# A [128, 128] bfloat16 identity and four columns of ones moved from the first SBUF pool to the third, in a one-core two-block transformer kernel

## The chip, the cores and the metric

The kernel runs on one core of a Trainium2 chip. The metric is the device time of one execution in microseconds. Before the change it is 2216.32 us, the median of three executions (2214.37 to 2220.98 us). Executions of one kernel lie close together, so a change of about 0.3%, some 7 us, is what a measurement of this kernel can tell from none.

TensorE multiplies a moving operand, streamed from SBUF, by a stationary operand (the weights) that was loaded into the array from SBUF before. The profile calls the two halves PE (the MATMUL) and PEld (the LDWEIGHTS), and they overlap. The notation `pm<-r,hi` names the PSUM tile that is written, then the moving operand, then the stationary one.

## The reference

Two blocks of a residual network act on 256 tokens of width 1024, in float32. Cut to what matters:

```python
def first_block(x, mem, ...):                     # depth 1
    h = x + 0.5 * rms_norm(swiglu(rms_norm(x)))                   # width 2816
    h = h + rms_norm(hybrid_mixer(rms_norm(h), w_in, ...) @ w_out)  # attention + delta rule
    h = h + rms_norm(memory_cross_attention(rms_norm(h), rms_norm(mem), ...))
    return h + 0.5 * rms_norm(swiglu(rms_norm(h)))

def second_block(x, p, ...):                      # depth 2
    for i in range(2):
        h = h + 0.5 * swiglu_2(rmsnorm(h), ...)
        h = h + hybrid_mixer_2(rmsnorm(h), w_in[i], ...)          # conv + state space
        h = h + 0.5 * swiglu_2(rmsnorm(h), ...)
        h = h + sigmoid(rmsnorm(h) @ ple_w_gate[i]) * (p[i] @ ple_w_proj[i])
    return rmsnorm(h, final_norm)
```

Nearly all the work is the products of a [256, K] activation with float32 weight matrices, 375 MB of them, each read once.

## The kernel before

**Split products.** Each float32 operand is kept as a pair of float32r tiles, a high part and the rest. `mm3` makes one 128 by 128 by 256 product from three matmuls: weights `wh` against `xh`, `wh` against `xl`, `wl` against `xh`. Each loads its own weights, `wh` twice.

**Weights.** `wunit` reads up to four [128, 256] blocks by one DMA of 512 KB into a tile `raw`, ScalarE writes the high part `hi` (L298), VectorE the rest `lo` (L299). There are four buffers of `raw`, three of `hi`, three of `lo`, of 4096 bytes a partition each, all in the pool `wp`. Block by block, `block` runs through two column halves and up to four K steps; the two halves lie 512 bytes apart, the steps 1024.

**Activations.** The tiles `s` ([128, 256] float32, 1024 bytes), `r` ([128, 2, 256] float32r, 2048 bytes: high part and rest) and `d` ([128, 2, 256] float32) are handed out by the arenas. `x[k]` in `mm3` is an `r` tile.

**Two places where the roles differ.** `preload` puts the first weights of the next projection into free `r` tiles instead of `hi` and `lo`; those matmuls read `pm<-r,r`. `proj_tok` takes the activations as the stationary operand and the weights as the moving one: `pm<-hi,r` and `pm<-lo,r`. `small_cols` multiplies by a narrow weight of 32 or 64 columns in a tile `smw`: `px<-r,smw`.

**What sets the order.** The Tile framework schedules the instructions by priorities; `AHEAD`, `PRELOAD` and `LATE` shift them. The five engines then run their queues in order.

**Where tiles lie.** The pools are laid out one behind the other in each partition of SBUF, in the order in which they are opened: `cst` (constants), `wp` (weights), `sc` (scratch), `arena` (activations), then the pools of a scope. The tiles of a pool are laid out in the order in which they are asked for, each rounded up to 32 bytes. In the built program before, by bytes in a partition: `cst` from 16512, the first `raw` at 25728, the first `hi` at 42112, the first `lo` at 54400, `sc` from 66688, the first `s` at 82240, the first `r` at 119104. All sizes in `wp` and in the arenas are multiples of 512, or pairs of 1024, so modulo 512 every weight tile lies at 128 and every arena tile at 320. This document calls the moving operand's address less the stationary one's, modulo 512, the **distance**: 192 for `pm<-r,hi` and `pm<-r,lo`, 320 for `pm<-hi,r`, 0 for `pm<-r,r`, and 0 or 256 for `px<-r,smw`, whose tile lies at 320 too.

The names that the change touches: `self.ones` (L161, four [128, 1] tiles, the moving operand of the sums of squares) and `self.identb` (L188, a [128, 128] bfloat16 identity, 256 bytes, the stationary operand in `fox` and `ssd` and for the masks of the delta rule).

Of the kernel before, what the change touches and what calls it, by code (L numbers as in the profile page):

```python
# [8 lines left out]
F32 = mybir.dt.float32  # L9
F32R = mybir.dt.float32r  # L10
BF16 = mybir.dt.bfloat16
# [4 lines left out]
P = 128  # L16
# [80 lines left out]
class Arena:  # L97


    def __init__(self, name, shape, dtype):  # L100
        self.name, self.shape, self.dtype = name, shape, dtype
        self.free, self.used, self.parts = [], {}, []
        self.n = self.peak = 0
# [33 lines left out]
class Net:  # L137
    def __init__(self, ctx, tc, a):
        self.tc, self.nc, self.a = tc, tc.nc, a
        nc = self.nc  # L140

        def pool(name, bufs, **kw):
            return ctx.enter_context(tc.tile_pool(name=name, bufs=bufs, **kw))

        self.cst = pool("cst", 1)
        self.wp = pool("wp", 3)
        self.scr, self.parts, self.pp = {}, [], []
        self.sc = pool("sc", 2)
        ap = pool("arena", 1)
        self.S = Arena("s", [P, S], F32)  # L150
        self.S.add(ap, 36)
        self.R = Arena("r", [P, 2, S], F32R)
        self.R.add(ap, 20)
        self.D = Arena("d", [P, 2, S], F32)
        self.D.add(ap, 0)
        self.pm = pool("pm", 4, space=bass.MemoryType.PSUM)
        self.px = pool("px", 4, space=bass.MemoryType.PSUM)

        self.con = self.cst.tile([P, NCON], F32, name="con")
        self.vec = self.cst.tile([P, NPACK], F32, name="vec")  # L160
        self.ones = {n: self.cst.tile([P, 1], F32, name=f"ones{n}") for n in (1, 128, 512, 1024)}  # L161
        nc.gpsimd.memset(self.ones[1], 1.0)
        for n in (128, 512, 1024):
            self.act(self.ones[n], self.ones[1], AF.Copy, scale=1.0 / n)
        self.h = self.start()
        self.ident = self.c("ident")
        nc.sync.dma_start(self.ident, a["con"][:, :P])
        self.ones_sq = self.cst.tile([P, P], F32, name="ones_sq")
        nc.gpsimd.memset(self.ones_sq, 1.0)
        self.mhalf = self.cst.tile([P, 16], F32, name="mhalf")  # L170
        self.cst.tile([P, 8], F32, name="pad")
        nc.gpsimd.memset(self.mhalf, -0.5)

    def constants(self):
        nc, a = self.nc, self.a
        nc.sync.dma_start(self.vec[:, 8:], a["pack"][:, 8:])
        nc.sync.dma_start(self.con[:, P:], a["con"][:, P:])
        tmps = [self.S.get() for _ in range(-(-NCONB // S))]
        for i, t in enumerate(tmps):
            n = min(S, NCONB - i * S)  # L180
            nc.sync.dma_start(t[:, :n], a["conb"][:, i * S:i * S + n])

        self.cb = self.cst.tile([P, NCONB], BF16, name="cb")
        for i, t in enumerate(tmps):
            n = min(S, NCONB - i * S)
            nc.gpsimd.tensor_copy(self.cb[:, i * S:i * S + n], t[:, :n])
        self.S.put(*tmps)
        self.identb = self.cst.tile([P, P], BF16, name="identb")  # L188
        nc.gpsimd.tensor_copy(self.identb, self.ident)
        self.maskT2 = self.cst.tile([P, 2, P], BF16, name="maskT2")  # L190
        nc.gpsimd.tensor_copy(self.maskT2, self.b("maskT")[:, None, :].to_broadcast([P, 2, P]))
        self.ident3 = self.b("ident3")[:96]
# [1283 lines left out]
```

## Time and profile before

| | |
|---|---|
| median of three executions | 2216.32 us |
| the profiled execution, its own time | 2218.59 us |
| its span, first instruction to last | 2216.8 us |
| PE busy | 2195.6 us (99%), 18672 matmuls |
| PEld busy | 2153.5 us (97%) |
| VectorE, ScalarE busy | 1558.2 us (70%), 1185.7 us (53%) |
| DMA | 379.44 MB, mean 171 GB/s |
| chain of work that ended last | PE 96%, VectorE 2%, ScalarE 1%, DMA 1% |

Around the span lie 1.8 us. A busy share says little for TensorE, since the matmuls overlap: one of 280 ns can follow the last after 113 ns. What tells its speed is how many start in a stretch of time: the windows view gives in brackets the instructions of each engine in each stretch, and its length by that count is the time from start to start, called the **pace** below. The timeline gives the start of each run of like instructions, and from one start to the next it gives the same.

### The profile page before, as it was taken

How to read it: one execution, taken by the hardware profiler on the slowest of the kernel's cores; microseconds unless marked ns; L12 is line 12 of the kernel's file. 1: busy time of each engine (PE TensorE's matmuls, PEld its weight loads, DVE VectorE, ACT ScalarE, POOL GpSimd, SP SyncE). 2: the span in 40 equal slices, each digit the busy share in tenths (PEclk: the TensorE clock that was granted, in tenths of full speed). 3: DMA queues.
4: the chain of work that ended last, by engine and by line, in shares of the span. 5: the costliest groups of instructions: out<-in, count | busy, mean ns of one | idle time of the engine just before them, and what ended most of it. 6: DMA issues, size and time to landing. Idle time of an engine off the chain costs nothing.

```text
span 2216.8 us, 45480 instructions
## 1 busy us (share of the span) xinstructions
PE 2195.6 (99%) x18672; PEld 2153.5 (97%) x18672; DVE 1558.2 (70%) x2608; ACT 1185.7 (53%) x2033; POOL 43.7 (2%) x54
## 2 busy tenths in 40 slices
PE   8999999999999999999999999999999999999998
PEld 8999997999999999998999999999999999999998
DVE  7756873667665766798766766676669876767666
ACT  6545633555444544567555555454457755645444
POOL 1000000000000000000000000000000000000000
PEclk9999997999999999999999999999999999999999
DMA  7565520535566556553455656656665436566563
GB/s 256 177 188 166 166 77 1 172 124 162 189 184 192 173 185 184 188 179 105 157 189 184 193 191 193 189 186 193 191 199 184 135 126 194 178 195 192 193 189 126
DMA packets 110369, 379.44 MB, mean 171 GB/s; under 512 B 12368, under 2 KB 17104, under 8 KB 110160
## 3 DMA queue, kind: packets, MB, share of 16 engines
q1 hardware_dynamic: 110160, 376.53, 53.6%
q8 instruction: 146, 2.39, 0.5%
q14 instruction: 63, 0.52, 0.1%
HBM read 375.43 MB, written 1.05 MB: 170 GB/s over the span
## 4 chain that ended last, share of the span: by engine, by line
PE 96%; DVE 2%; ACT 1%; DMA 1%; issue 0%; POOL 0%; SPq 0%; DVEq 0%; ACTq 0%; POOLq 0%
PE pm L266 84%; PE px L266 11%; PE px L269 1%; DVE lo L299 0%; DVE s L260 0%; DMA raw<-in_ffn_w_gate_dram 0%; DMA raw<-in_ple_w_gate_dram 0%; ACT hi L298 0%; DMA raw<-in_ffn_wu_dram 0%; ACT d L263 0%; PE pm L269 0%; ACT L263 0%; DVE r L260 0%; DVE w L254 0%; DVE w L260 0%
## 5 line engine op out<-in xcount | busy, mean ns | idle before, releaser
L266 PE MATMUL pm<-r,hi 128*128 128x256 f32 x10640 | 1864.0, 280 | 7.5 <-ACT hi L298 5.7
L266 PEld LDWEIGHTS pm<-r,hi 128*128 128x128 f32 x10640 | 1625.1, 189 | 9.8 <-ACT hi L298 5.7
L266 PE MATMUL pm<-r,lo 128*128 128x256 f32 x5320 | 1485.3, 279 | 0.0
L299 DVE TENSOR_TENSOR lo<-raw,hi 128x1024 fp32r<-128x1024 f32 (+1 forms) x718 | 860.9, 1199 | 488.9 <-ACT hi L298 485.6
L298 ACT CAST hi<-raw 128x1024 fp32r<-128x1024 f32 (+1 forms) x718 | 739.3, 1030 | 732.7 <-PE pm L266 576.7
L266 PEld LDWEIGHTS pm<-r,lo 128*128 128x128 f32 x5320 | 1002.1, 188 | 1.2 <-issue 0.7
L277 ACT CAST r<-w 128x256 fp32r<-128x256 f32 x136 | 54.5, 403 | 60.4 <-DVE w L254 60.3
L254 DVE TENSOR_TENSOR t<-pm,rb 128x512 f32<-128x512 f32 (+1 forms) x132 | 80.4, 635 | 0.2
L263 ACT ACTIVATE r<-s,vec 128x256 fp32r<-128x256 f32 x136 | 66.0, 504 | 21.4 <-DVE s L260 17.9
L263 ACT ACTIVATE sq<-s 128x256 f32<-128x256 f32 x152 | 60.4, 411 | 28.1 <-DVE s L254 19.8
L260 DVE SCALAR_TENSOR_TENSOR s<-pm,vec,s 128x255 f32<-128x255 f32 x144 | 68.9, 479 | 2.8
L260 DVE SCALAR_TENSOR_TENSOR r<-s,vec,r 128x256 fp32r<-128x256 f32 x136 | 65.3, 498 | 4.9 <-ACT r L263 4.4
L266 PE MATMUL px<-r,hi 128*128 128x256 f32 x384 | 66.9, 279 | 0.0
L278 DVE TENSOR_TENSOR r<-w,r 128x256 fp32r<-128x256 f32 x136 | 57.0, 421 | 8.1
L266 PEld LDWEIGHTS px<-r,hi 128*128 128x128 f32 x384 | 58.6, 189 | 0.0
L266 PE MATMUL px<-r,lo 128*128 128x256 f32 x192 | 53.5, 278 | 0.0
L414 POOL TENSOR_TENSOR rs<-rv,mhalf 128x2 f32<-128x2 f32 x26 | 23.4, 900 | 1505.0 <-DVE rv L412 1505.0
L263 ACT ACTIVATE w<-t 128x256 f32<-128x256 f32 x132 | 48.1, 409 | 7.2 <-DVE t L254 7.2
L254 DVE TENSOR_TENSOR w<-w,t 128x256 f32<-128x256 f32 x132 | 50.1, 418 | 0.3 <-ACT w L263 0.2
L266 PE MATMUL px<-d,d 128*64 128x128 f32 (+2 forms) x384 | 42.7, 291 | 0.3 <-DVE d L254 0.2
L257 DVE TENSOR_TENSOR acc<-acc,sq 128x256 f32<-128x256 f32 x94 | 39.4, 419 | 4.6 <-ACT sq L263 1.9
L263 ACT ACTIVATE d<-px,nac 128x128 f32<-128x128 f32 x128 | 36.5, 376 | 3.1 <-PE px L266 2.8
(231 smaller groups left out, 1369.2 us busy)
## 6 DMA issues: line engine op xcount, KB each, us to landing
raw<-in_w_in_dram SPq DMA_DIRECT2D x188, 512.0 KB, 3.7
raw<-in_ffn_wg_dram SPq DMA_DIRECT2D x88, 512.0 KB, 4.4
raw<-in_ffn_wu_dram SPq DMA_DIRECT2D x88, 512.0 KB, 4.3
raw<-in_ffn_wd_dram SPq DMA_DIRECT2D x80, 512.0 KB, 4.0
raw<-in_ffn_w_up_dram SPq DMA_DIRECT2D x44, 512.0 KB, 4.5
raw<-in_ffn_w_gate_dram SPq DMA_DIRECT2D x43, 512.0 KB, 4.5
raw<-in_ffn_w_down_dram SPq DMA_DIRECT2D x40, 512.0 KB, 3.8
raw<-in_m_w_out_dram SPq DMA_DIRECT2D x32, 512.0 KB, 4.3
```

Of the source, the lines that this page charges most:

```text
L254: self.nc.vector.tensor_tensor(out=out, in0=a, in1=b, op=ALU.mult)
L257: self.nc.vector.tensor_tensor(out=out, in0=a, in1=b, op=ALU.add)
L260: self.nc.vector.scalar_tensor_tensor(out=out, in0=a, scalar=s, in1=b, op0=op0, op1=op1)
L263: self.nc.scalar.activation(out, a, f, **kw)
L266: self.nc.tensor.matmul(out, lhsT=lhsT, rhs=rhs, start=start, stop=stop)
L269: self.nc.tensor.transpose(out, a, self.ident[:k, :k])
L277: nc.scalar.copy(hi, src)
L278: nc.vector.tensor_tensor(out=lo, in0=src, in1=hi, op=ALU.subtract)
L298: nc.scalar.copy(o, r)
L299: nc.vector.tensor_tensor(out=d, in0=r, in1=o, op=ALU.subtract)
L414: self.nc.gpsimd.tensor_tensor(out=r, in0=v, in1=self.mhalf[:, :2], op=ALU.pow)
```

## The change

`self.ones` and `self.identb` are asked for from `sc` instead of `cst`.

```diff
@@ -158,7 +158,7 @@
-        self.ones = {n: self.cst.tile([P, 1], F32, name=f"ones{n}") for n in (1, 128, 512, 1024)}
+        self.ones = {n: self.sc.tile([P, 1], F32, tag=f"ones{n}", name=f"ones{n}", bufs=1) for n in (1, 128, 512, 1024)}
@@ -185,7 +185,7 @@
-        self.identb = self.cst.tile([P, P], BF16, name="identb")
+        self.identb = self.sc.tile([P, P], BF16, name="identb", bufs=1)
```

`cst` shrinks by 4 times 32 and 256 bytes, 384 in all, and `sc` grows by as much. In the built program after, the weight tiles lie 384 bytes lower (first `hi` at 41728, 256 modulo 512), and the arenas and all behind them where they were (320 modulo 512). The distance becomes 64 for `pm<-r,hi` and `pm<-r,lo`, 448 for `pm<-hi,r`; for `pm<-r,r` it stays 0. Scratch tiles ahead of `identb` lie 256 bytes lower. The instructions of all five engines, their order and their waits are the same as before, row for row; only addresses differ.

## Rows read from the trace of the kernel before

**Rows 1.** The page's totals: busy time of each engine, the granted clock by fortieths, and the shares of the chain that ended last.

```profile
PE 2195.6 (99%) x18672; PEld 2153.5 (97%) x18672; DVE 1558.2 (70%) x2608; ACT 1185.7 (53%) x2033; POOL 43.7 (2%) x54
...
PEclk9999997999999999999999999999999999999999
...
PE 96%; DVE 2%; ACT 1%; DMA 1%; issue 0%; POOL 0%; SPq 0%; DVEq 0%; ACTq 0%; POOLq 0%
```

**Rows 2.** Groups of instructions by line and shape, for TensorE: names, shapes, count, then busy us, mean ns of one, and idle time before them with what ended it. The float32r products and those that touch the moved tiles.

```profile
L266 PE MATMUL pm<-r,hi 128*128 128x256 f32 x10640 | 1864.0, 280 | 7.5 <-ACT hi L298 5.7 <-ACT r L263 1.1 <-DVE r L260 0.7
...
L266 PE MATMUL pm<-r,lo 128*128 128x256 f32 x5320 | 1485.3, 279 | 0.0
...
L266 PE MATMUL px<-r,hi 128*128 128x256 f32 x384 | 66.9, 279 | 0.0
...
L266 PE MATMUL px<-r,lo 128*128 128x256 f32 x192 | 53.5, 278 | 0.0
...
L266 PE MATMUL pm<-hi,r 128*128 128x256 f32 x192 | 33.7, 279 | 0.0
...
L266 PE MATMUL pm<-lo,r 128*128 128x256 f32 x96 | 26.8, 279 | 0.0
...
L266 PE MATMUL pm<-r,r 128*128 128x256 f32 x168 | 22.8, 287 | 0.3 <-ACT r L263 0.3
...
L266 PE MATMUL px<-ones,acc 128*128 128x1 f32 x152 | 20.4, 227 | 0.6 <-DVE acc L257 0.6
...
L266 PE MATMUL px<-maskT,identb 128*128 128x256 bf16 x64 | 15.8, 273 | 0.0
...
L266 PE MATMUL px<-ones,sq 128*128 128x1 f32 x72 | 11.0, 256 | 1.4 <-ACT sq L263 1.4
...
L266 PEld LDWEIGHTS <-identb 128*128 128x128 bf16 x88 | 8.6, 98 | 6.5 <-issue 5.6
```

**Rows 3.** Busy time of each engine in ten stretches of unbroken projections, with the count of instructions in brackets, the granted clock, the DMA share and GB/s.

```profile
62.00:202.00 140.00, 139.97 (x1188) 139.77 (x1188) 88.45 (x121) 66.76 (x96) 0.26 (x1) 1.00 0.59 181
541.00:721.00 180.00, 179.99 (x1528) 179.64 (x1526) 115.74 (x161) 86.60 (x131) 0.70 (x1) 1.00 0.61 188
738.00:921.00 183.00, 183.00 (x1557) 183.00 (x1556) 119.17 (x160) 89.60 (x130) 2.57 (x1) 1.00 0.60 186
941.00:1009.00 68.00, 68.00 (x581) 68.00 (x580) 62.49 (x114) 46.29 (x73) 0.00 (x0) 1.00 0.57 180
1066.00:1152.00 86.00, 86.00 (x761) 86.00 (x761) 58.16 (x84) 43.58 (x61) 0.00 (x0) 1.00 0.58 185
...
1277.00:1451.00 174.00, 173.42 (x1531) 173.22 (x1529) 117.15 (x165) 89.48 (x134) 0.00 (x0) 1.00 0.62 196
1483.00:1659.00 176.00, 176.00 (x1555) 176.00 (x1554) 117.27 (x159) 89.80 (x130) 2.59 (x1) 1.00 0.62 193
1679.00:1744.00 65.00, 65.00 (x576) 65.00 (x576) 61.83 (x112) 46.07 (x73) 0.00 (x0) 1.00 0.59 187
...
1928.00:2010.00 82.00, 82.00 (x726) 82.00 (x725) 56.62 (x85) 42.39 (x63) 0.70 (x1) 1.00 0.61 192
2012.00:2180.00 168.00, 168.00 (x1484) 168.00 (x1484) 110.31 (x150) 82.46 (x119) 0.00 (x0) 1.00 0.62 192
```

**Rows 4.** The instructions of line 266 on PE in one stretch of 20 us at each of two places, and in one of 6 us: count, then shortest, median and longest duration in ns, and first and last start.

```profile
L266 PE MATMUL pm<-r,hi x115: 281/281/281, 619.8 to 639.9; 128*128 128x256 f32 x115
...
L266 PE MATMUL pm<-r,hi x119: 276/276/276, 1299.9 to 1319.9; 128*128 128x256 f32 x119
...
L266 PE MATMUL pm<-r,r x48: 281/283/283, 1470.1 to 1475.8; 128*128 128x256 f32 x48
```

**Rows 5.** The timeline of PE around a run of preloaded weights: start us, length us, what, count.

```profile
1469.44 0.39 PE L266 MATMUL pm<-r,hi 128*128 128x256 f32 x2
...
1470.12 5.92 PE L266 MATMUL pm<-r,r 128*128 128x256 f32 x48
1475.88 0.40 PE L266 MATMUL pm<-r,hi 128*128 128x256 f32 x2
...
1476.23 0.40 PE L266 MATMUL pm<-r,hi 128*128 128x256 f32 x2
...
1480.00 0.40 PE L266 MATMUL pm<-r,hi 128*128 128x256 f32 x2
...
1480.36 0.40 PE L266 MATMUL pm<-r,hi 128*128 128x256 f32 x2
```

**Rows 6.** The same view around a run of narrow weights.

```profile
1673.80 0.40 PE L266 MATMUL pm<-r,hi 128*128 128x256 f32 x2
...
1675.21 1.99 PE L266 MATMUL px<-r,smw 128*64 128x256 f32 x16
1677.03 0.40 PE L266 MATMUL pm<-r,hi 128*128 128x256 f32 x2
```

**Rows 7.** The same view of a product with the weights as the moving operand (`proj_tok`).

```profile
487.97 0.40 PE L266 MATMUL pm<-hi,r 128*128 128x256 f32 x2
...
491.85 0.40 PE L266 MATMUL pm<-hi,r 128*128 128x256 f32 x2
```

**Rows 8.** The same view of bfloat16 matmuls of 256 columns, two of them with the identity as weights.

```profile
1016.22 0.27 PE L266 MATMUL px<-maskT,identb 128*128 128x256 bf16 x1
...
1016.66 0.27 PE L266 MATMUL px<-maskT,identb 128*128 128x256 bf16 x1
```

## The prediction

> **What bounds the kernel now.** I read the totals and the chain first: PE is busy for 99% of the span and makes 96% of the chain that ended last, at the full granted clock nearly throughout [rows 1]. So the time is the number of matmuls by their pace, and little else. The groups say which matmuls: 10640 + 5320 + 384 + 192 + 192 + 96 + 168 = 16992 float32r ones of 256 columns, with 8 us of idle time before them in all [rows 2]. The reader should distrust their mean of 280 ns and go to the counts of the windows. There the same work runs at two paces. In the stretches 62:202, 541:721, 738:921 and 941:1009, 571 us hold 1188 + 1528 + 1557 + 581 = 4854 matmuls, 117.6 ns each. In the six stretches from 1066 on, 751 us hold 6633, 113.2 ns each [rows 3]. (A window counts a matmul that it cuts, so both are a little low: start by start I read 117.8 and 113.3.) The clock reads 1.00 in all of them, and the DMA share is 0.57 to 0.62 in both kinds, so neither explains it. The durations show the paces as well: 281 ns in a slow stretch, 276 in a fast one, each to the nanosecond for over a hundred in a row [rows 4].
>
> Both paces stand at the same distance of 192. So the distance alone does not fix the pace: it is a rhythm that the stream falls into and keeps. Three groups of rows show what goes with it:
> - Distance 0. The preloaded weights: 48 matmuls from 1470.12 to 1475.88, 5.76 us, are 120.0 ns each, and 283 ns long. The stream before them ran fast (1469.44 to 1470.12, 0.68 us for six), the stream behind them, at distance 192 again, runs slow: from 1475.88 to 1476.23 three take 0.35 us, and from 1480.00 to 1480.36 still 0.36 [rows 4, 5].
> - Narrow weights. Sixteen matmuls with 64 columns of weights, at distances 0 and 256 in turn, take 1.82 us, 113.8 ns each, in the middle of a slow stream: 1673.80 to 1675.21 is 1.41 us for twelve, 117.5 ns [rows 6]. So the moving stream alone asks for 113.3 at most, and only beside a full weight load does it get slower.
> - Distance 320: from 487.97 to 491.85 are 33 matmuls of `proj_tok`, 3.88 us, 117.6 ns, the slow pace [rows 7].
>
> I read this as a collision of the two reads of SBUF. The moving stream covers 1024 bytes while the weight load covers 512, so modulo 512 one overtakes the other once in each matmul. Where it does so depends on the distance and on which of the two is ahead, and what it costs on whether the weight load still ends in time. At distance 0 they start and end together, and each matmul pays 6.7 ns over the fast pace. At 192 they meet in the middle: the fast pace pays nothing that shows over the narrow weights, the slow one pays 4.5 ns.
>
> The Trainium skill speaks against this: its page "TensorE: Matmul & The Clock Gate", section "Step-by-step: what each phase is for", gives TensorE two independent read ports and says that loading the next weights takes no read bandwidth from the running matmul. By that rule the change would do nothing; rows 5 disagree, with 120.0 against 113.3 ns for the same shape and type, and what it would make of the time is the third rival below.
>
> **The change, part by part.** No instruction, order or wait changes, so every term is a pace.
> - *The projections.* 10640 + 5320 + 576 = 16536 matmuls go from distance 192 to 64. The slow pace holds the 4854 counted above and, start by start in the mixed stretches that are left, some 1900 more: 6750 together, 40%. The price at distance 64 no row shows; the bounds are the rows at 0 and at 192. Lower bound: all at the fast pace, 6750 x 4.5 = 30 us gained (4.44 by the unrounded paces). Upper bound: all at 120.0, which costs 9950 x 6.7 + 6750 x 2.2 = 81 us. I take the lower bound. At 64 the moving stream starts 64 bytes ahead of the load, so the two no longer start in the same place, which at distance 0 is the one thing that sets it apart; and it catches the load from behind later than at 192, when most of the load is done and little of it is left to hold up. It is the weaker half of the argument that the slow pace goes; that nothing gets worse than at 192 is the stronger.
> - *`proj_tok`.* 288 matmuls go from 320 to 448. Bounds 113.3 and 120.0 against a slow 117.6: -1.2 to +0.7 us. I take 0.
> - *Preloaded weights.* 168 stay at 0: no change.
> - *The identity.* 88 bfloat16 matmuls with `identb` as weights, of which 64 follow others at 0.11 us [rows 2, 8]. Even 6.7 ns either way for each is 0.6 us. 0.
> - *The ones.* 224 short matmuls (152 and 72 of them) [rows 2] wait for their weights, not for their one column, and the weights move with the scratch. Same bounds: 1.5 us either way. 0.
> - *What a faster TensorE asks for.* In the fast stretches DMA runs at 185 to 196 GB/s, ScalarE and VectorE at up to 71% and 95% of a stretch [rows 3], and PE is busy for all but 0.6 us. So the fast pace is already fed, by the very loops that would now run at it throughout. In 941:1009 and 1679:1744, the same stage at either pace, VectorE has 62 us of work in 68 and 65. Nothing new is late next.
>
> Sum, on the profiled execution: 2218.6 - 30.0 = 2188.6 us. It is 2.3 us above the median of the three, so I predict 2187 us.
>
> **The rivals.**
> 1. *Distance 64 is too near to 0 (slower).* If what counts is that both reads start in the same or the next piece of SBUF, 64 may fall to the same 120.0 as 0, and the time is 2216 + 81 = 2297 us; if only the slow pace takes all, 9950 x 4.5 = 44 us, 2260. It decides from where the mean pace passes 115.1 ns, today's mean of the two. For it: 64 is nearer to 0 than any distance that a row shows with wide weights. Against it: the collision at 0 is of two streams that start level, and a lead of 64 bytes grows from the first column on, as the moving stream is twice as fast. Chance 0.25.
> 2. *Both paces stay, and the stalls deal them out anew.* The run at 1470 shows how a few matmuls choose the pace for microseconds [rows 5]; rows 3 that it then holds for 180 us. With another distance each stretch could fall the other way. All between 2187 and 2260 us is open then, 4.4 us for each thousand matmuls, and about 2216 as likely as any. For it: both 192 and 320 show the slow pace [rows 3, 7]. Chance 0.20.
> 3. *The address doesn't matter*, and the change does not do what its arithmetic says: the pace at 1470 has another cause, and the time stays at 2216 us. For it: one distance with two paces. Chance 0.07.
> 4. *The fast pace is itself a collision.* bfloat16 matmuls of 256 columns follow each other after 0.44 us for four, 110 ns [rows 8]. If 64 freed the rest, 16536 x 3.3 = 55 us more would go, to some 2133 us. Against it: narrow weights, with less to collide, still need 113.8. Chance 0.03.
>
> **How the numbers follow.** The forecast, all of the projections at the fast pace, has 0.45. Its own range is 2181 to 2194 us. The range reaches from 2180 to 2262 us: it holds the forecast, rivals 2 and 3, and the milder half of rival 1, about 0.84. Faster by over 0.3% (below 2209.7): 0.45 + 0.03 + two fifths of rival 2, 0.56. Within 0.3%: rival 3 and 0.15 of rival 2, 0.10. Slower: rival 1 and 0.45 of rival 2, 0.34. The 0.3% is about what a measurement of this kernel can tell from no change.
>
> **What would show it.** In the windows after, the stretches of the first feed-forward parts, which lie before 1010 us now and are slow, should hold matmuls at 113.3 ns, so 62:202 some 1235 instead of 1188; the durations there should read 276. If rival 1 is right, 1300:1320 reads 281 or 283. If rival 2 is right, both numbers stand somewhere in the profile, and in other places than now. If 3, all rows stay, the slow stretches in the same places. The prediction is wrong if any long projection still shows a pace above 114.

## The result, and the profile after

The changed kernel takes 2231.6 us (median of 11), the kernel before 2217.9 us beside it (median of 11): a ratio of 1.0061, with a 95% interval of 1.0041 to 1.008. It is slower by 0.6%, 13.7 us. The forecast was faster by 1.3%, 2187 us; the measured time lies inside the range, and on the other side of no change. It lies inside because the range was wide enough to hold rival 2, and rival 2 is what happened.

The page after, first the lines that answer to [rows 1], then those that answer to [rows 2]:

```profile
PE 2203.2 (99%) x18672; PEld 2163.5 (97%) x18672; DVE 1559.0 (70%) x2608; ACT 1185.5 (53%) x2033; POOL 43.4 (2%) x54
...
PEclk9999997999999999999999999999999999999999
...
PE 96%; DVE 2%; ACT 1%; DMA 1%; issue 0%; POOL 0%; SPq 0%; DVEq 0%; ACTq 0%; POOLq 0%
...
L266 PE MATMUL pm<-r,hi 128*128 128x256 f32 x10640 | 1876.5, 280 | 6.7 <-ACT hi L298 5.8
...
L266 PE MATMUL pm<-r,lo 128*128 128x256 f32 x5320 | 1486.8, 280 | 1.3 <-DVE lo L299 1.3
```

Little in these lines says that the kernel has changed: the tenths of the clock, the chain and the counts are the same, and the mean of the largest group is 280 ns in both. Only the busy times of PE and PEld grew by more than 1 us, by 7.6 and 10.0 us. The counts of the windows tell more. These are windows of the kernel after, with the columns of [rows 3]; a window lies up to 7 us away from its partner there, where the stream has moved:

```profile
62.00:202.00 140.00, 139.97 (x1189) 139.77 (x1188) 88.58 (x120) 66.21 (x96) 0.26 (x1) 1.00 0.59 182
539.50:719.50 180.00, 179.99 (x1527) 179.66 (x1527) 115.76 (x161) 86.65 (x131) 0.70 (x1) 1.00 0.61 188
738.00:921.00 183.00, 183.00 (x1556) 183.00 (x1556) 118.87 (x159) 89.13 (x130) 2.73 (x2) 1.00 0.60 186
941.00:1009.00 68.00, 68.00 (x581) 68.00 (x581) 62.99 (x112) 47.14 (x73) 0.00 (x0) 1.00 0.58 182
1065.00:1151.00 86.00, 86.00 (x732) 86.00 (x732) 55.20 (x81) 42.16 (x59) 0.00 (x0) 1.00 0.57 183
...
1279.00:1453.00 174.00, 173.13 (x1528) 172.94 (x1527) 117.10 (x164) 89.59 (x134) 0.00 (x0) 1.00 0.63 197
1484.50:1660.50 176.00, 176.00 (x1556) 176.00 (x1555) 117.34 (x159) 89.83 (x130) 2.59 (x1) 1.00 0.63 193
1681.00:1746.00 65.00, 65.00 (x554) 65.00 (x553) 60.08 (x106) 44.44 (x69) 0.00 (x0) 1.00 0.57 182
...
1935.00:2017.00 82.00, 82.00 (x726) 82.00 (x726) 56.29 (x84) 42.41 (x63) 0.69 (x1) 1.00 0.61 192
2019.00:2187.00 168.00, 168.00 (x1485) 168.00 (x1484) 110.02 (x149) 82.64 (x120) 0.00 (x0) 1.00 0.62 192
```

The four slow stretches of [rows 3] still hold the same number of matmuls: 1189 for 1188 in 62:202, where the forecast wanted some 1235. Of the fast ones, two fell to the slow pace: the window from 1065 holds 732 instead of 761, and the one from 1681 holds 554 instead of 576. No third pace has come up. The durations agree. In the 20 us after 620 and after 1300 they are, of the kernel after (as [rows 4]):

```profile
L266 PE MATMUL pm<-r,hi x114: 278/280/281, 619.9 to 639.8; 128*128 128x256 f32 x114
```

```profile
L266 PE MATMUL pm<-r,hi x119: 275/276/277, 1299.8 to 1319.9; 128*128 128x256 f32 x119
```

Where a stream falls to the other pace can be seen matmul by matmul. This is the timeline of PE where the stream of 767 projections begins that [rows 3] shows from 1066 on, of the kernel before:

```profile
1064.91 0.49 PE L266 MATMUL px<-s,d 128*128 128x128 f32 x2
1065.24 0.22 PE L266 MATMUL px<-T,selp 96*128 96x128 bf16 x1
1065.27 0.37 PE L266 MATMUL pm<-r,hi 128*128 128x256 f32 x1
...
1065.59 0.39 PE L266 MATMUL pm<-r,hi 128*128 128x256 f32 x2
...
1066.27 0.39 PE L266 MATMUL pm<-r,hi 128*128 128x256 f32 x2
```

And the same of the kernel after:

```profile
1063.43 0.49 PE L266 MATMUL px<-s,d 128*128 128x128 f32 x2
1063.76 0.22 PE L266 MATMUL px<-T,selp 96*128 96x128 bf16 x1
1063.79 0.37 PE L266 MATMUL pm<-r,hi 128*128 128x256 f32 x1
...
1064.11 0.40 PE L266 MATMUL pm<-r,hi 128*128 128x256 f32 x2
...
1066.23 0.40 PE L266 MATMUL pm<-r,hi 128*128 128x256 f32 x2
```

The instructions ahead of the stream are the same, at the same distances in time to within 0.02 us. Then six matmuls take 0.68 us before (1065.59 to 1066.27, 113.3 ns each), and after 18 take 2.12 us (1064.11 to 1066.23, 117.8 ns each). The pace is fixed in the first few matmuls and then holds for 86 us.

Laid side by side, start by start, the two profiled executions differ like this. Call the time from one start to the next a **pitch**; the pace is the mean of many. Of the 16632 pitches between two float32r matmuls of [rows 2] that are below 130 ns in both kernels, 6712 are 116 ns or longer before and 9762 after. That is 3050 more at the slower pace, 3050 x 4.45 = 13.6 us, and the sum of these pitches grew by 13.6 us. All the rest gives 6.7 us back, so that the spans differ by 6.9 us only.

Most of what is given back goes with the clock and not with the layout. Between the streams that begin at 281 and at 389 us, where matmuls of other shapes stand, 89.1 us pass before and 84.7 after, 4.3 us less. The granted clock there is not the same in the two executions; before, then after:

```profile
340.00:400.00 60.00, 60.00 (x303) 47.54 (x304) 22.57 (x71) 20.86 (x63) 1.65 (x1) 0.69 0.06 20
```

```profile
340.00:400.00 60.00, 59.91 (x341) 49.24 (x340) 25.54 (x76) 23.78 (x70) 1.65 (x1) 0.77 0.09 30
```

With the two levels of the clock, 1.2 and 2.4 GHz, a mean of 0.69 in these 60 us is an estimated 37 us at the lower level (2 x 0.31 x 60), and 0.77 an estimated 28; half of the difference is 4.7 us, near the 4.3 seen. The kernel e1 below, which has the tiles moved as in the change and the same 0.69 here as before, also has the same 303 matmuls in this window. How long it lasts differs between executions of one kernel too: the mean granted clock of the 11 executions after runs from 0.988 to 0.993, and the profiled one, with 0.992 and 2225.5 us, is among the quickest. The medians differ by 13.7 us, close to what the projections make.

### The profile page after: what moved, and what is told of

It reads as the page before. It is cut to its first block, busy times and chain, and to the rows that moved or that the text cites. A ratio compares the mean times of both kernels' runs of the same rounds, so it can differ in the third digit from the quotient of the medians.

```text
span 2223.7 us, 45480 instructions
## 1 busy us (share of the span) xinstructions
PE 2203.2 (99%) x18672; PEld 2163.5 (97%) x18672; DVE 1559.0 (70%) x2608; ACT 1185.5 (53%) x2033; POOL 43.4 (2%) x54
## 4 chain that ended last, share of the span: by engine, by line
PE 96%; DVE 2%; ACT 1%; DMA 1%; issue 0%; POOL 0%; SPq 0%; DVEq 0%; ACTq 0%; POOLq 0%
PE pm L266 85%; PE px L266 11%; PE px L269 1%; DVE lo L299 0%; DVE s L260 0%; DMA raw<-in_ffn_w_up_dram 0%; DMA raw<-in_ple_w_gate_dram 0%; DMA raw<-in_ffn_wu_dram 0%; DVE r L260 0%; PE pm L269 0%; ACT d L263 0%; ACT hi L298 0%; ACT L263 0%; DVE acc L257 0%; DVE w L254 0%
```

## The experiments

Three questions were asked in turn: whether the distance decides or something else that moved with the tiles; which distances are good; and what picks one of the two paces for a stream. Each ratio is to executions of the kernel before that were taken together with it.

### Does the distance decide?

The theories: the distance between activations and weights decides; or the paces have nothing to do with addresses (rival 3); or the new places of the moved tiles do it.

**e1_moved_d192**: the change with a gap that brings the distance back to 192.

```diff
         self.identb = self.sc.tile([P, P], BF16, name="identb", bufs=1)
+        self.sc.tile([P, 32], F32, name="gap", bufs=1)
```

> The change as it is, plus an unused gap of 128 bytes at the end of the scratch pool: the identity and the ones stay behind the weights, the distance goes back to 192. Theory A (the distance decides which of the two paces, 113.3 or 117.8 ns, a stretch runs at): back to before, 2218 us within 7, and slow and fast stretches where they were before, so 1066:1152 at 113.3 ns. Theory B (the paces have nothing to do with addresses, and each stretch falls into one or the other by small differences of time at its start): somewhere between 2187 and 2260 us, at no known place. Theory C (the places of the moved tiles decide, since their short matmuls stand ahead of the long streams): 2232 us as after the change, 1066:1152 at 117.8 ns.

Measured: 2217.5 us, 0.999 (0.9976 to 1.0005). The tiles lie where the change puts them, and the loss is gone.

**e2_ident_d0**: the identity alone moved, and a gap of 64 bytes (`[P, 16]`) behind it: distance 0.

> The identity alone behind the weights, plus a gap of 64 bytes: distance 0 for the projections. Theory A: all long stretches at the 120.0 ns of the preloaded weights, about 2297 us (2285 to 2305). Theory B: only 113.3 and 117.8 ns to be seen, 2187 to 2260 us. Theory C: as B, since the ones stay where they were, near before.

Measured: 2291.9 us, 1.0329 (1.0308 to 1.035). Matmul durations and weight loads of 20 us from 620 on, of this kernel (its lines are one further down):

```profile
L267 PE MATMUL pm<-r,hi x113: 283/283/283, 619.8 to 640.0; 128*128 128x256 f32 x113
```

```profile
L267 PEld LDWEIGHTS pm<-r,hi x113: 192/192/192, 619.8 to 640.0; 128*128 128x128 f32 x113
```

The 283 ns are those of the preloaded weights in [rows 4], now in nearly every projection: 16033 of the 16646 pitches below 130 ns are 120 ns. That the address matters is shown: the only thing that differs from the kernel before is where tiles lie.

**e3_pad_d320** (the kernel before with a gap of 128 bytes) and **e4_ident_d448** (the identity alone moved) set two more distances.

> Before, plus a gap of 128 bytes at the end of the scratch pool, nothing moved: distance 320. Theory A: 320 is -192, so the two paces are the same two, and the share of the slow one may differ from 40%; 2187 to 2260 us. If a collision from the other side costs the same, 2218 us. Theory B: 2187 to 2260 us. Theory C: before, 2218 us within 7.

> The identity alone behind the weights, no gap: distance 448, which is -64. Theory A: if only how near the distance is to 0 counts, as after the change, 2232 us; a pace above 117.8 ns somewhere would show that the side matters. Theory B: 2187 to 2260 us, only 113.3 and 117.8 ns. Theory C: between before and after.

Measured: 2233.6 us, 1.006 (1.0039 to 1.008) at 320; 2220.1 us, 0.9987 (0.997 to 1.0005) at 448. The long streams of both show 113.3 and 117.8 ns and no other pace. So 320 stands with 64, and 448 with 192: they are 256 apart.

### Which distances are good?

**f1_ident_d64** (identity alone moved, gap of 128 bytes) sets the changed kernel's distance by other moves; **f2_moved_d128** (the change, gap of 64), **f3_pad_d256** (before, gap of 64) and **f4_ones_d384** (the ones alone moved, gap of 64) test whether 256 is the period.

> The identity alone moved, with a gap of 128 bytes behind it: distance 64 as in the change, by other moves and with the ones at their old place. If the distance deals out the paces: only 113.3 and 117.8 ns, the slower one in some 60 % of the projections, about 2232 us, 1.006 of before. If the moved ones, or where the tiles lie in full, have a part in it: back towards 2218.

> The change with a gap of 64 bytes: distance 128. Measured so far: 0 gives 2292, 64 and 320 give 2232 and 2234, 192 and 448 give 2218 and 2220 us. If what counts is the distance modulo 256, 128 and 384 give the same time to within 0.3 %. If it is the distance modulo 512, nothing ties the two together. In either case no pace but 113.3 and 117.8 ns, so 2185 to 2262 us.

> The kernel before with a gap of 64 bytes: distance 256. If what counts is the distance modulo 256, this is distance 0: 120.0 ns in every projection and about 2292 us. If it is the distance modulo 512, 256 is as far from 0 as can be: 113.3 and 117.8 ns in some mixture, 2185 to 2262 us.

> The ones alone moved, with a gap of 64 bytes: distance 384. Modulo 256 this is 128: the time of the distance 128 to within 0.3 %. Modulo 512 it is a case of its own: 113.3 and 117.8 ns in some mixture, 2185 to 2262 us.

Measured: 2231.1, 2274.8, 2292.9 and 2276.0 us. Distance 64 is the changed kernel again to 0.5 us, 256 is 0 again to 1 us, and 384 is 128 again to 1.3 us. At 0, 64, 128 and 192 the time repeats after 256 bytes. The kernels that agree differ in which tiles moved and in where the weights lie (at distance 64 they lie at 128, 256 and 384 modulo 512), so neither of these decides by itself.

**g1_pad_d224** (before, gap of 32), **g2_pad_d288** (before, gap of 96), **g3_ones_d352** (ones moved, gap of 32) and **g4_moved_d160** (the change, gap of 96) fill in the odd multiples of 32.

> The kernel before with a gap of 32 bytes: distance 224. Measured so far, modulo 256: 0 gives 2292, 64 gives 2232, 128 gives 2275, 192 gives 2218 us. If SBUF answers in pieces of 64 bytes and only the piece counts, 224 is 192: 2218 us, 113.3 and 117.8 ns. If the distance itself counts, it lies between 192 and 256: some 2218 to 2292 us. If the pieces are of 32 bytes and reads whose distance is an odd number of them never meet, only 113.3 ns is left: 2187 us.

> The kernel before with a gap of 96 bytes: distance 288, 32 modulo 256. Pieces of 64 bytes: as distance 0, 2292 us and 120.0 ns. The distance itself: between 0 and 64, 2232 to 2292 us. Odd pieces of 32 bytes that never meet: 113.3 ns alone, 2187 us.

> The ones alone moved, with a gap of 32 bytes: distance 352, 96 modulo 256. Pieces of 64 bytes: as 64, 2232 us with 113.3 and 117.8 ns. The distance itself: between 64 and 128, 2232 to 2275 us. Odd pieces of 32 bytes that never meet: 2187 us.

> The change with a gap of 96 bytes: distance 160. Pieces of 64 bytes: as 128, 2275 us. The distance itself: between 128 and 192, 2218 to 2275 us. Odd pieces of 32 bytes that never meet: 2187 us.

Measured: 2262.3, 2242.6, 2292.3 and 2262.2 us. No theory held for all four. Pieces of 64 bytes fail at each (2262 for 2218, 2243 for 2292, 2292 for 2232, 2262 for 2275), and so do pieces of 32 bytes that never meet. That the time lies between its neighbours holds at 32, 160 and 224 and fails at 96, which is as slow as 0 though 64 and 128 are both quicker.

In the window 1530:1650 of 120 us, the column of counts is the one to read; e2 (0), g2 (32), g3 (96), f2 (128) and g1 (224), one after the other:

```profile
1530.00:1650.00 120.00, 120.00 (x1002) 120.00 (x1002) 77.58 (x103) 56.58 (x85) 0.00 (x0) 1.00 0.58 183
```

```profile
1530.00:1650.00 120.00, 120.00 (x1031) 120.00 (x1030) 77.00 (x104) 58.70 (x85) 0.00 (x0) 1.00 0.61 186
```

```profile
1530.00:1650.00 120.00, 120.00 (x1002) 120.00 (x1002) 77.82 (x103) 56.68 (x85) 0.00 (x0) 1.00 0.58 183
```

```profile
1530.00:1650.00 120.00, 120.00 (x1014) 120.00 (x1013) 77.86 (x102) 56.81 (x83) 0.00 (x0) 1.00 0.59 183
```

```profile
1530.00:1650.00 120.00, 120.00 (x1016) 120.00 (x1016) 77.43 (x103) 57.43 (x84) 0.00 (x0) 1.00 0.59 184
```

The whole map, with the paces read start by start:

| distance mod 256 | kernels | median us | ratio to before | paces (means of twelve pitches), ns |
|---|---|---|---|---|
| 0 | e2, f3 | 2291.9, 2292.9 | 1.033, 1.034 | 120.0 |
| 32 | g2 | 2242.6 | 1.011 | 116.7 |
| 64 | changed, f1, e3 | 2231.6, 2231.1, 2233.6 | 1.006 each | 113.3 and 117.8, 58 to 69% slow |
| 96 | g3 | 2292.3 | 1.033 | 120.0 |
| 128 | f2, f4 | 2274.8, 2276.0 | 1.026 | 118.7, in two stages 120.0 |
| 160 | g4 | 2262.2 | 1.019 | 117.3 and 118.7 |
| 192 | before, e1, e4 | 2217.9, 2217.5, 2220.1 | 1, 0.999, 0.999 | 113.3 and 117.8, 37 to 45% slow |
| 224 | g1 | 2262.3 | 1.021 | 118.3 |

Only 64 and 192 have streams at the fast pace. At 0 nearly every single pitch is 120 ns; at 96 they run from 115 to 125 ns and come to the same mean. The rows 32, 96, 160 and 224 rest on one kernel each; that they too repeat after 256 bytes was not tried. The kernel before stands at the best of the eight.

### What picks the pace of a stream?

A **stream** is an unbroken run of projections, and its **entry** the short matmuls right ahead of it. At many entries stand the two matmuls of the helper `spread`, each of which shows as two of `px<-con,rs`. In the traces of distance 64 and 192 (modulo 256) the long streams behind all four in a row were slow, and those with a projection between the two `spread` matmuls were mostly fast. Four kernels move only that. **h1_split2** works on the kernel before:

```diff
+        self.nsp = getattr(self, "nsp", 0) + 1
...
-            self.mm(ps[:, t * P:(t + 1) * P], r[:, j:j + 1].to_broadcast([P, P]), self.ident)
+            p = {16: -3, 18: -3}.get(self.nsp, 0) * t
+            with self.tc.high_priority(p) if p else nullcontext():
+                self.mm(ps[:, t * P:(t + 1) * P], r[:, j:j + 1].to_broadcast([P, P]), self.ident)
```

**h2_after_split2** is the same in the changed kernel; **h3_join3** and **h4_after_join3** have `{24: 4, 26: 4, 32: 4}` in its place, which puts the two matmuls together ahead of three streams.

> The kernel before, with two matmuls moved by one place: where the streams of 1500 and 1557 projections begin (at 541 and 738 us), the two spread matmuls that stand together there get one projection between them, as ahead of the streams that begin at 1276, 1482 and 2011 us. If the matmuls at the entry fix the pace: both streams go from 117.8 to 113.3 ns, 3057 x 4.45 ns = 13.6 us less, about 2206 us, 0.994. If what else runs in a stage fixes it (its weights, transfers, other engines): no change. If it is chance at each entry: anything between, and no clean change of both.

> The changed kernel with the same two matmuls moved. The entry: 13.6 us less than the changed kernel, 2218 us, 1.000 of before, with both streams at 113.3 ns. The stage: 2232 us, 1.006.

> The reverse, in the kernel before: ahead of the three streams that begin at 1276, 1482 and 2011 us (1551 + 1559 + 1551 projections) the two spread matmuls are put together. The entry: all three go from 113.3 to 117.8 ns, 4661 x 4.45 ns = 20.7 us more, about 2239 us, 1.009. The stage: no change.

> The reverse in the changed kernel: the entry 20.7 us more than it, about 2252 us, 1.0155 of before, with nearly every projection at 117.8 ns; the stage 2232 us.

Measured: h1 2216.1 us, 0.9992 (0.9976 to 1.0009), and h2 2234.3 us, 1.0072 (1.005 to 1.0094): splitting does nothing, and both streams stay slow at either distance. h3 2233.9 us, 1.0078 (1.0057 to 1.0099), and h4 2247.5 us, 1.0134 (1.0115 to 1.0153): 15.6 us more than before, and 15.9 more than the changed kernel, where 20.7 were expected. In the traces all three joined streams went slow, at both distances. The stream at 1482 says little, since it is slow in three of the ten traces where it was not joined; the two others never are, and they alone make 3102 x 4.45 = 13.8 us. Windows inside them, of h3 and then of h1, where these three are as before:

```profile
1300.00:1445.00 145.00, 145.00 (x1234) 145.00 (x1233) 93.03 (x126) 69.29 (x102) 0.00 (x0) 1.00 0.60 185
1510.00:1650.00 140.00, 140.00 (x1191) 140.00 (x1190) 89.67 (x120) 67.07 (x98) 0.00 (x0) 1.00 0.61 186
2045.00:2185.00 140.00, 140.00 (x1191) 140.00 (x1190) 88.71 (x116) 65.83 (x95) 0.00 (x0) 1.00 0.61 186
```

```profile
750.00:915.00 165.00, 165.00 (x1403) 165.00 (x1402) 105.23 (x139) 80.79 (x116) 2.57 (x1) 1.00 0.61 186
1300.00:1445.00 145.00, 144.82 (x1277) 144.58 (x1275) 96.23 (x133) 74.63 (x112) 0.00 (x0) 1.00 0.64 198
1510.00:1650.00 140.00, 140.00 (x1238) 140.00 (x1237) 91.40 (x121) 71.20 (x103) 2.59 (x1) 1.00 0.63 193
2045.00:2185.00 140.00, 140.00 (x1237) 139.99 (x1236) 90.27 (x123) 70.00 (x100) 0.02 (x1) 1.00 0.64 193
```

1234 for 1277 in the first, 1191 for 1238 in the second. The window 750:915 of h1 is one of the streams that was to become fast: 1403 in 165 us, 117.6 ns. So the entry can make a stream slow, and the stage of work is not what made it fast; but the split is not enough to make it fast.

**h5_bf16_entry** (kernel before) and **h6_after_bf16_entry** (changed kernel) try the one kind of entry that was always followed by the fast pace at 192, that of the timelines above, ahead of the two longest slow streams:

```diff
+        if self.nsp in (16, 18):
+            self.mm(ps[:, S:S + P], self.identb, self.identb)
         return ps[:, :S]
```

> The kernel before, with one short bfloat16 matmul (identity by identity, into unused columns) put between the two spread matmuls and each of the streams that begin at 541 and 738 us, as the short bfloat16 matmul with selp as weights stands ahead of the streams at 1065 and 1800 us, which are at 113.3 ns in every kernel of distance 192 or 448 so far. If the last matmul ahead of a stream fixes its pace at a given distance: both streams go to 113.3 ns, 13.6 us less, about 2205 us, 0.994. If the pace of the stream before lives on through a few short matmuls: both stay at 117.8 ns, 2218 us.

> The same two short matmuls in the changed kernel. The streams behind the selp matmul are at 117.8 ns in every kernel of distance 64 or 320 so far: if entry and distance fix the pace together, both streams stay slow, 2232 us, 1.006 of before. If the short matmul works whatever the distance: 2218 us.

Measured: 2220.8 us, 1.0014 (0.9997 to 1.0032), and 2230.5 us, 1.006 (1.0035 to 1.0085). Both streams stayed slow in both. The timeline of PE in h5, where the first of them begins:

```profile
537.54 0.60 PE L266 MATMUL px<-con,rs 128*128 128x128 f32 x4
537.98 0.22 PE L266 MATMUL px<-identb 128*128 128x128 bf16 x1
538.01 0.36 PE L266 MATMUL pm<-r,lo 128*128 128x256 f32 x1
538.21 0.40 PE L266 MATMUL pm<-r,hi 128*128 128x256 f32 x2
...
538.57 0.40 PE L266 MATMUL pm<-r,hi 128*128 128x256 f32 x2
...
538.92 0.28 PE L266 MATMUL pm<-r,hi 128*128 128x256 f32 x1
```

From 538.21 to 538.92 six matmuls take 0.71 us: slow from the start, with the short bfloat16 matmul right ahead. So a short bfloat16 matmul in the last place does not pick the fast pace. It is not the same one as at 1065 us (128 partitions and the identity here, 96 partitions and `selp` there), and the rest of the entry differs too.

The twelve traces at these distances, by the longer streams and those that tell the distances apart (starts are those of the kernel before; slow share of each stream's matmuls, read start by start), show what the distance does all the same:

| streams (start us, projections) | six kernels at 192 | six kernels at 64 |
|---|---|---|
| 22 (292), 541 (1500), 738 (1557) | slow in all | slow in all |
| 1192, 1927 (709 each) | fast in all | fast in all |
| 1276, 2011 (1551 each) | fast, but for the joined one | fast, but for the joined one |
| 411 (192), 1065 and 1800 (767 each) | fast in all | slow in all |
| 281 (168) | fast in all | 44% slow in all |
| 60 (1200) | slow in three | slow in all |
| 940 (572) | slow in five | slow in all |
| 1482 (1559) | slow in two, one of them joined | slow in three, one of them joined |
| 1678 (572) | slow in four | slow in four |

The same twelve traces tell what an entry does. Here are all streams of 500 projections and more that begin behind `spread`, by the pace of the last seven unbroken projections ahead of the entry. It is a count over traces; only h1 to h6 changed entries on purpose.

| the two `spread` matmuls | pace ahead | streams | fast behind | slow behind |
|---|---|---|---|---|
| together | fast | 7 | 0 | 7 |
| together (four with the short matmul of h5 and h6 behind) | slow | 19 | 0 | 19 |
| a projection between | fast | 42 | 42 | 0 |
| a projection between | slow | 28 | 12 | 16 |

One case of the first row, the stream at 541 us in e1, where the pace ahead was fast (540.70 to 541.38, six in 0.68 us) and that behind is slow (542.17 to 542.88, six in 0.71):

```profile
540.70 0.39 PE L267 MATMUL pm<-r,hi 128*128 128x256 f32 x2
...
541.38 0.39 PE L267 MATMUL pm<-r,hi 128*128 128x256 f32 x2
541.61 0.60 PE L267 MATMUL px<-con,rs 128*128 128x128 f32 x4
...
542.17 0.40 PE L267 MATMUL pm<-r,hi 128*128 128x256 f32 x2
...
542.88 0.28 PE L267 MATMUL pm<-r,hi 128*128 128x256 f32 x1
```

So a fast pace lived through every entry with a projection between, at either distance, and through none with the two together; a slow pace ended at some of the former and at none of the latter. The four split entries of h1 and h2 all had the slow pace ahead, which is the case that can come out either way. Behind `selp` the distance alone decides: the pace ahead was slow in all 24 cases, and the stream is fast in all 12 at 192 and slow in all 12 at 64.

So a part of the loss is fixed by place: 192 + 767 + 767 + 0.44 x 168 = 1800 matmuls x 4.45 ns = 8.0 us of the 14 are streams that fall to the slow pace at 64 every time. The rest comes from streams that can fall either way, among them one of 1200 that never was fast at 64. Such streams can make executions of one kernel differ, and the clock does too: e2, with one pace in all projections, took from 2288.6 us at a mean granted clock of 0.993 to 2299.0 at 0.988. How much of the spread of the kernel before (2200.7 to 2228.2 us in 11 executions) each of the two makes was not measured.

No kernel beat the one before by more than its interval.

## Why the prediction was wrong

- **What bounds the kernel.** Right. The pace of the float32r matmuls makes 13.6 us between the profiled executions, close to the 13.7 of the medians, with the same instructions and chain.
- **The collision depends on the distance; rival 3.** Right that the pace does: distance 0 gave 120.0 ns everywhere, and 192 set again gave the old time. The Trainium skill, page "TensorE: Matmul & The Clock Gate", section "Step-by-step: what each phase is for", gives TensorE two independent read ports and says that loading the next weights takes no read bandwidth from the running matmul. By that rule the distance would not matter, and these runs do not agree: a change of the distance alone cost 3.3% (e2). That it is a collision of two reads, and where in the chip, no run shows.
- **Modulo 512, and "too near to 0".** Wrong. The time repeats after 256 bytes, and nearness to 0 is not what counts: 96 pays 120.0 on the mean, as 0 does, and 32 pays 116.7. The picture of one read that overtakes the other once in a matmul fell with it. With the right period the answer stood in the trace: [rows 7] show distance 320, which is 64 modulo 256, at the slow pace.
- **The term "The projections".** This is the step that failed. Its price at 64 lay between 30 us gained and 81 lost, and I took the lower bound, because "the slow pace goes"; the prediction called that the weaker half of its argument. The slow pace did not go. It took 3050 matmuls more, 13.6 us lost in the profiled executions, where 30 us were to be gained. The stronger half, that nothing gets worse than at 192, failed too: no pace got worse, but the share of the slow one did. A slip of the upper bound changes little: 16536 less 6750 are 9786 matmuls, not 9950, and the bound is 80 us.
- **Rival 2, both paces stay and are dealt out anew.** Right, with 0.20 of the chance, and its sign to read: "both numbers stand somewhere in the profile, and in other places than now". Its price of 4.4 us for each thousand matmuls is what was measured. What I gave it too little for was my own sentence that a distance with two paces does not fix the pace; [rows 3] show two paces at 192 and [rows 7] the slow one at 320, and no row shows a wide-weight distance that has the fast pace alone. Taking 64 as such a distance went beyond the rows.
- **Other terms at 0** (`proj_tok`, preloaded, identity, ones, a faster TensorE). No run tests them one by one. What the profiled executions differ by outside the projections is 6.7 us in the other direction; 4.3 of them stand where the lower clock lasted longer in the execution before, which the prediction had no term for.
- **What stays open.** Why the distances have the paces that they have; why the streams behind `selp` are fast at 192 and slow at 64; and what ends a slow pace at some entries with a projection between. Shown is that two `spread` matmuls put together make a stream slow at both distances (the streams at 1276 and 2011 us in h3 and h4). That the pace ahead lives on is half of it: in the table of entries a fast one does where a projection stands between, and none does where the two stand together.

## What to carry to other kernels

When a dense stream of matmuls shows two paces at one clock, compute the distance between the moving operand and the weights modulo 256 bytes, and try the neighbouring distances with a gap tile: one gap of 64 bytes made this kernel 3.4% longer, with no instruction changed. What was measured are float32r matmuls of 256 columns with a load of 128 by 128 weights each; other shapes and types were not tried. Do not extrapolate from one bad distance to a good one; of eight only two have the fast pace, and these two also have a slow one. A layout change of any kind, a small constant moved for another reason, can therefore cost time without any other sign: 0.6% for the change here, 3.4% at the worst distance. The distance should be checked after each. And where two profiled executions are compared, compare their granted clocks first.

## What was not expected of the hardware

- The pace depends on the distance modulo 256 bytes, and follows no simple order within it: 120.0, 116.7, 113.3/117.8, 120.0, 118.7, 117.3/118.7, 113.3/117.8, 118.3 ns in steps of 32. That it repeats was tried at the multiples of 64.
- At 64 and 192 a stream has two lasting rhythms: three matmuls in 340 ns, or in 353.3 ns. Either holds for over 1500 matmuls (175 to 183 us).
- At distance 0 each of 113 weight loads lasts 192 ns, together with a pitch of 120.0 ns. But the longer load is not what goes with that mean pitch: at 96 the loads of the same stretch have a median of 187 ns, and in the slow pace at 192 one of 190:

```profile
L267 PEld LDWEIGHTS pm<-r,hi x112: 187/187/193, 619.9 to 639.9; 128*128 128x128 f32 x112
```

```profile
L266 PEld LDWEIGHTS pm<-r,hi x114: 187/190/192, 620.0 to 639.9; 128*128 128x128 f32 x114
```
